# A hybrid decoder step: GLU, last projections and decode scores in one ordered list, and another row order for the decode score loads

## The chip, the core and the metric

The kernel runs on one NeuronCore of a Trainium2 chip. TensorE (PE) multiplies matrices into PSUM, VectorE (DVE), ScalarE (ACT) and GpSimd (POOL) do elementwise work, and SyncE's queue (SP) issues all DMA transfers of this kernel. Each engine works through its own instructions in order. The metric is the device time of one execution in microseconds (us); lower is better. All arithmetic is float32, with matmul operands split into a high and a low part, so that a product takes three matmul passes.

## The reference, cut to what matters

One layer of a decoder for a prompt of 1024 tokens and a decode batch of 8 sequences with 4 new tokens each. A projection gives `[x_ssm | z_ssm | q | k | v | z_attn]`. The state-space branch ends with a GLU; the attention branch of the decode rows attends to a cache of 1024 rows under three patterns.

```python
proj = _rmsnorm(h, norm_in_g) @ w_in
...
gl = g @ w_glu.astype(jnp.float32) + b_glu.astype(jnp.float32)
y_s = gl[..., :D_SSM] * jax.nn.sigmoid(gl[..., D_SSM:])
y_s = (y_s * jax.nn.silu(z_s.astype(jnp.float32))).astype(h.dtype)
y_s = _rmsnorm(y_s, norm_ssm_g)
...
offs = jnp.arange(window // dil + 1) * dil
idx = (l_ - t_ + jnp.arange(t_))[:, None] - offs[None, :]
...
s = jnp.einsum('bthe,btkhe->bhtk', q, kg) * (HEAD_DIM ** -0.5)
...
out = jnp.concatenate([y_s, y_a], axis=-1) @ w_out
```

with `DILATED_PATTERNS = ((128, 1), (512, 4), (2048, 16))`, `DEC_BATCH = 8`, `DEC_SEQ = 4`.

## The kernel before

The work runs in stages. First the prompt is normalised and transposed (`xT`), then the input projection goes block by block (`in_proj(blk)`, 12 blocks of 256 columns) between the eight groups of the state-space scan (`ssm(o)`). The change concerns the stage behind that.

**GLU** (lines 718 to 773). `w_glu` is loaded in four tiles `wst` and split into `wg`. For each pair `s0` of eight row groups and each of four column tiles `ct`, PE does 24 matmuls (L748) into two PSUM tiles, ACT takes tanh (L753) into `gb_`, of which there is one buffer, DVE gates (L754, L755), ACT squares (L759), and POOL adds the squares into `acc` (L760). The last two need `gb_`, so the next tanh waits for POOL's addition.

**Decode scores** (lines 811 to 838). For each batch `b` six tiles of 128 cache rows are loaded into `ct` (three buffers): tile 0 (L791), tile 1 (L793) and tiles 6 to 9 (L797). Tile 0 is transposed on PE (L822), split into `kh` and `kl`, and multiplied with the queries (L828, L829). For the other five POOL multiplies the tile with the query rows `dq` (L802, `dot`), and DVE reduces the product per head into `scd` (L803). `dq` has one buffer; its load (L835) spreads the four query rows over 128 partitions. `kh`, `kl` and the products share three buffers `dm`. The tiles are loaded so that query j stands on partitions 32j to 32j+31:

```python
SY.dma_start(c, src[b, 0:512, :].rearrange("(m r) c -> r m c", r=16)[0:DS])
...
SY.dma_start(c, src[b, 512:1024, :].rearrange("(m r j) c -> m j r c", r=32, j=DS)[t - 6])
...
SY.dma_start(qt, d_pd[:, b, 1024:1536].unsqueeze(1).to_broadcast([DS, 32, 512]))
```

**Last projections.** Blocks 6 and 10 (`REST_BLOCKS`, six groups of 24 matmuls each, L313, weights split at L141 and L142, results stored to `d_k` and `d_ga` at L381 and L373), then four tiles of `w_out`, then the softmax over the scores (`decode_ops`: transposes L914, softmax L921 to L967, transposes back L979), then block 11.

**What sets the order.** The code up to here is written straight down, and the framework's own scheduler interleaves it: it places each instruction on its engine, and SP's transfers too, by its own estimate. `decode_ops` and the attention behind it (`values_ops`, `scores_ops`, `micro_ops`, `out_ssm_ops`) are lists of steps of a class `Plan`: each step has an engine, a cost, a priority, the steps it needs and the buffers it takes and gives (`tokens`). `Plan.run` goes through the list as if each engine took that long, always takes the step that can start first (the smaller priority among equals), and emits the steps in the order of their starts. In the attention this order is fixed on PE, DVE, ACT and POOL (`manual_schedule`).

Of the kernel before, what the change touches and what calls it, by code (L numbers as in the profile page):

```python
# [95 lines left out]
BANKS = {"fo": 3, "tp": 4, "ss": 7, "ops": 3, "kt": 3}  # L96
# [6 lines left out]
def hymba_kernel(ctx: ExitStack, tc: tile.TileContext, I, O):  # L103
# [600 lines left out]
    fin = [rp]  # L704

# [9 lines left out]
    wg = wgo.tile([128, 2, 4, 1024], F32R, tag="wg", name="wg")  # L715
    for k in range(4):
        s = st.tile([128, 1024], F32, tag="st", name="wst")
        SY.dma_start(s, I["w_glu"][k * 128:(k + 1) * 128, :])
        split(wg[:, 0, k, :], wg[:, 1, k, :], s)

    bg, hb = wk([128, 8], "bg"), wk([128, 4], "hb")
    SY.dma_start(bg, I["b_gluT"])
    V.tensor_scalar(hb, bg[:, 4:8], 0.5, 1.0, op0=OP.mult, op1=OP.mult)
    for k in range(4):
        SY.dma_start(z[:, k], d_y[k])
    sums = ps_tile([128, 8], "so")
    dsum = ps_tile([128, NT], "so")
    all1 = wk([128, 128], "all1")
    GP.memset(all1, 1.0)
    for s0 in range(0, 8, 2):  # L730
        w, ts = W if s0 < DS else NC, slice(s0, s0 + 2)
        yh, yl = (wk([128, 4, 2, W], n, F32R, b) for n, b in (("yh", 2), ("yl", 1)))
        for k in range(0, 4, 1 if s0 == 0 else 2):
            k = slice(k, k + (1 if s0 == 0 else 2))
            split(yh[:, k], yl[:, k], z[:, k, ts])
        yT = yh, yl
        acc = wk([128, 2, W], "acc", bufs=1)[:, :, :w]
        for ct in range(4):
            gt = wk([128, 2, W], "gt", bufs=3)[:, :, :w]
            SY.dma_start(gt, d_gs[ct, :, ts, :w])  # L740
            pp = []
            for hf, tag in enumerate(("ss", "ss")):
                p = ps_tile([128, 512], tag)[:, :2 * w].rearrange("p (s k) -> p s k", k=w)
                i = 0
                c = 512 * hf + 128 * ct
                for kt in range(4):
                    for a, b in PASSES:
                        T.matmul(p, wg[:, b, kt, c:c + 128], yT[a][:, kt, :, :w], start=(i == 0), stop=(i == 11))  # L748
                        i += 1
                pp.append(p)  # L750
# [54 lines left out]
    def query():  # L805
        return dk([128, 512], "dq", bufs=1)
# [825 lines left out]
```

## Time and profile before

| | us |
|---|---|
| time, median of 3 runs | 816.28 (814.58 to 818.41) |
| the profiled execution's own time | 816.68 |
| its span in the trace | 814.8 |
| PE busy | 703.5 (86% of the span) |
| DVE / ACT / POOL busy | 561.2 / 363.3 / 347.0 |
| chain that ended last, by kind | PE 37%, DMA 28%, DVE 17%, ACT 5%, POOL 4% |

The profile gives each engine's busy time, the clock that PE was granted (1.00 is 2.4 GHz, 0.50 is 1.2 GHz), the chain of work that ended last, and for each instruction what ended its wait. The largest single entry of the chain is the load of decode cache tiles, `ct<-in_cache_k_dram`, with 12.8% of the span. The stage of the change lies between 324 and 535 us.

### The profile page before, as it was taken

The numbers are of one execution on the slowest core, as the hardware profiler recorded it, in microseconds if no ns is written. First come the engines' busy times: TensorE is split into PE (matmuls) and PEld (weight loads), VectorE is DVE, ScalarE is ACT, GpSimd is POOL, SyncE is SP. The second block draws the span as 40 slices with busy tenths as digits, with TensorE's granted clock in tenths as the row PEclk, the third lists the DMA queues.
The fourth block names the chain that finished last, engine by engine and source line by source line (L and its number), as shares of the span: only waits on it lengthen the run. The fifth ranks groups of instructions, "written<-read, shape, count | busy, mean of one in ns | idle before, by whom it ended". The sixth has DMA issues, their size and how long they took to land.

```text
span 814.8 us, 12780 instructions
## 1 busy us (share of the span) xinstructions
PE 703.5 (86%) x4286; PEld 634.6 (78%) x4286; DVE 561.2 (69%) x1249; ACT 363.3 (45%) x814; POOL 347.0 (43%) x315
## 2 busy tenths in 40 slices
PE   7999989598989999587767668989989999989996
PEld 6999878588978899576767657867757777778896
DVE  5995787879786762444435355649789999996286
ACT  6653244223425244322212222228667787772163
POOL 2506663544654410133433334016567687740022
PEclk9999999798999999796898878989999999999999
DMA  8424142322332444554434354368898788305423
GB/s 282 162 79 139 37 135 85 119 63 67 110 123 93 156 132 147 151 143 160 127 119 142 114 175 139 108 183 243 251 254 247 218 234 242 101 6 181 132 84 130
DMA packets 77362, 118.38 MB, mean 145 GB/s; under 512 B 14544, under 2 KB 42704, under 8 KB 77296
## 3 DMA queue, kind: packets, MB, share of 16 engines
q1 hardware_dynamic: 77296, 117.56, 46.8%
q8 instruction: 34, 0.56, 0.3%
q14 instruction: 32, 0.26, 0.1%
HBM read 85.73 MB, written 30.62 MB: 143 GB/s over the span
## 4 chain that ended last, share of the span: by engine, by line
PE 37%; DMA 28%; DVE 17%; issue 5%; ACT 5%; POOL 4%; SPq 3%; DVEq 0%; POOLq 0%; ACTq 0%
DMA ct<-in_cache_k_dram 13%; PE mm L313 13%; PE mm L293 4%; DMA ct<-in_cache_v_dram 4%; PE ss L293 3%; PE tp L293 3%; PE fo L1418 3%; DMA wst<-in_w_in_dram 3%; PE so L684 2%; POOL dm L802 2%; DVE pm L1269 2%; PE ops L1323 2%; DVE vl L1107 2%; DMA dq<-d_pd 2%; DVE pl L1315 2%
## 5 line engine op out<-in xcount | busy, mean ns | idle before, releaser
L313 PE MATMUL mm<-xT,win 128*128 128x352 f32 x1440 | 262.9, 338 | 23.4 <-DVE eq L380 16.7
L313 PEld LDWEIGHTS mm<-xT,win 128*128 128x128 f32 x1440 | 242.4, 198 | 28.0 <-issue 14.6
L802 POOL TENSOR_TENSOR dm<-ct,dq 128x512 f32<-128x512 f32 x40 | 52.5, 1312 | 124.2 <-DMA ct<-in_cache_k_dram 80.4
L803 DVE TENSOR_REDUCE scd<-dm 128x8 f32<-128x512 f32 x40 | 27.4, 684 | 78.0 <-POOL dm L802 78.0
L748 PE MATMUL ss<-yh,wg 128*128 128x272 f32 (+1 forms) x256 | 56.4, 317 | 19.8 <-DVE z L754 17.1
L1289 POOL TENSOR_SCALAR pm<-pm,rd 128x128 f32<-128x128 f32 (+3 forms) x64 | 52.0, 818 | 39.1 <-DVE rd L1285 27.6
L748 PEld LDWEIGHTS ss<-yh,wg 128*128 128x128 f32 x256 | 46.5, 217 | 22.4 <-DVE z L754 18.7
L142 DVE SCALAR_TENSOR_TENSOR win<-wst,gin,win 128x256 fp32r<-128x256 f32 x96 | 55.2, 617 | 11.0 <-ACT win L141 10.7
L141 ACT ACTIVATE win<-wst,gin 128x256 fp32r<-128x256 f32 x96 | 43.7, 502 | 33.7 <-DMA wst<-in_w_in_dram 29.8
L1281 ACT ACTIVATE pm<-pm,mn 128x128 f32<-128x128 f32 (+3 forms) x64 | 49.2, 770 | 15.3 <-DVE mn L1269 14.9
L1315 DVE TENSOR_TENSOR pl<-tp,ph 128x512 fp32r<-128x512 f32 (+1 forms) x80 | 49.7, 628 | 5.7 <-ACT ph L1312 5.4
L1418 PE MATMUL fo<-wo,gh 128*128 128x512 f32 x192 | 51.1, 408 | 0.0
L293 PE MATMUL mm<-win,xT 128*128 128x256 f32 x384 | 50.4, 286 | 0.1
L1308 PE MATMUL tp<-ident,pm 128*128 128x128 f32 x288 | 47.0, 283 | 1.5 <-DVE mn L1269 1.2
L293 PEld LDWEIGHTS mm<-win,xT 128*128 128x128 f32 x384 | 46.9, 189 | 0.5 <-ACT xT L138 0.4
L1312 ACT ACTIVATE ph<-tp 128x512 fp32r<-128x512 f32 (+1 forms) x80 | 42.9, 543 | 2.7 <-PE tp L1308 1.2
L1269 DVE CUSTOM_DVE_ANT_0 pm<-ss,maskp 128x512 f32<-128x512 f32 (+2 forms) x64 | 36.9, 580 | 9.6 <-DMA qt<-d_q 4.8
L1266 PE MATMUL ss<-ka,qt 128*128 128x512 f32 (+2 forms) x96 | 38.1, 398 | 4.3 <-DMA ka<-d_k 2.4
L1308 PEld LDWEIGHTS tp<-ident,pm 128*128 128x128 f32 x288 | 35.6, 145 | 7.5 <-DVE mn L1269 1.9
L1418 PEld LDWEIGHTS fo<-wo,gh 128*128 128x128 f32 x192 | 35.4, 194 | 6.6
L1103 ACT ACTIVATE vh<-ct 128x512 fp32r<-128x512 f32 x48 | 30.0, 626 | 23.1 <-DMA ct<-in_cache_v_dram 10.9
L379 ACT ACTIVATE eq<-mm 64x352 fp32r<-64x352 f32 (+1 forms) x48 | 21.5, 448 | 41.7 <-DVE eq L380 20.6
(399 smaller groups left out, 1584.7 us busy)
## 6 DMA issues: line engine op xcount, KB each, us to landing
wst<-in_w_in_dram SPq DMA_DIRECT2D x24, 512.0 KB
ct<-in_cache_k_dram SPq DMA_DIRECT2D x48, 256.0 KB
ct<-in_cache_v_dram SPq DMA_DIRECT2D x48, 256.0 KB
xt<-in_x_prompt_dram SPq DMA_DIRECT2D x8, 512.0 KB
wst<-in_w_out_dram SPq DMA_DIRECT2D x8, 512.0 KB
xres<-in_x_prompt_dram SPq DMA_DIRECT2D x8, 512.0 KB
qt<-d_q SPq DMA_DIRECT2D x16, 256.0 KB
qw<-d_q SPq DMA_DIRECT2D x32, 128.0 KB
```

What stands on the lines that cost most here:

```text
L141: S.activation(hi, src, AF.Copy, scale=scale)
L142: V.scalar_tensor_tensor(lo, src, scale, f(hi), op0=OP.mult, op1=OP.subtract)
L293: T.matmul(out, lhs(a, kt), w(b, kt)[:, c0:c0 + cn], start=(n == 0), stop=(n == 3 * ktn - 1))
L313: T.matmul(p, w(b, kt)[:, c * 128:c * 128 + 128], x(a, kt), start=(n == 0), stop=(n == 23))
L748: T.matmul(p, wg[:, b, kt, c:c + 128], yT[a][:, kt, :, :w], start=(i == 0), stop=(i == 11))
L802: GP.tensor_tensor(out=m, in0=kt, in1=qt, op=OP.mult)
L1269: V.tensor_tensor_reduce(out=x.pm[:, 512 * c:512 * c + w], in0=x.p[c][:, :w], in1=maskp[:, (7 - i) * 128 + 512 * c:(7 - i) * 128 + 512 * c ...
L1281: S.activation(x.pm[:, :n], x.pm[:, :n], AF.Exp, scale=-1.0, bias=x.mn[:, nch - 1:nch], accum_out=x.dn)
L1289: a = op(PO, 0.02 + n * 0.0012, lambda: GP.tensor_scalar(x.pm[:, :n], x.pm[:, :n], x.rd, 1.0, op0=OP.mult, op1=OP.mult), pr, [a], give=["rd"])
L1308: T.transpose(x.p[:, n * 128:n * 128 + 128], o.rows[2 * m + u].pm[:, j * 128:j * 128 + 128], ident)
L1315: V.tensor_tensor(out=x.l[:, :w], in0=x.p[:, :w], in1=f(x.h[:, :w]), op=OP.subtract)
L1418: T.matmul(o.f[hf], o.g[u][:, i, k], wo[0][:, j, 2 * u + k, hf * 512:hf * 512 + 512], start=(u + k + n == 0), stop=(u + k + n == 4))
```

## The change

Three things change together.

1. **Row order of the decode score tiles.** Query j now stands on each partition 4m+j. Tiles 6 to 9 are then 128 neighbouring rows, tile 1 and the query rows are loaded with the 32 as the outer count, and the places that undo the order (`ev`, `tr3`, `copy3`, the constant `sel3`) follow. `ct` has five buffers in place of three.
2. **One list of steps.** GLU, decode scores, blocks 6, 10 and 11, the `w_out` tiles and `decode_ops` become steps of one `Plan`, with costs and priorities, and the order is fixed on all five queues, SP's too.
3. **PSUM.** The pool of eight equal banks is opened before the GLU instead of after block 11; the GLU may hold up to four banks (`gl`).

The instructions are otherwise the same: same matmuls, same elementwise operations, same bytes.

```diff
+BANKS = {"fo": 3, "tp": 4, "ss": 7, "ops": 3, "kt": 3, "mm": 3, "gl": 4}
 REST_BLOCKS = (6, 10)
+LAST_BLOCK = 11
...
+    KT = 5
     def cache_tile(src, b, t):
-        c = dk([128, 512], "ct", bufs=3) if fin[0] else gk([128, 512], "ct", bufs=CT)
+        c = dk([128, 512], "ct", bufs=KT) if fin[0] else gk([128, 512], "ct", bufs=CT)
         if t == 0:
             SY.dma_start(c, src[b, 896:1024, :])
         elif t == 1:
-            SY.dma_start(c, src[b, 0:512, :].rearrange("(m r) c -> r m c", r=16)[0:DS])
+            SY.dma_start(c, src[b, 0:512, :].rearrange("(m r) c -> m r c", r=16)[:, 0:DS])
         elif t < 6:
             SY.dma_start(c, src[b, 510 + t:1024:4, :])
         else:
-            SY.dma_start(c, src[b, 512:1024, :].rearrange("(m r j) c -> m j r c", r=32, j=DS)[t - 6])
+            SY.dma_start(c, src[b, 128 * t - 256:128 * t - 128, :])
...
-        SY.dma_start(qt, d_pd[:, b, 1024:1536].unsqueeze(1).to_broadcast([DS, 32, 512]))
+                SY.dma_start(x.q, d_pd[:, b, 1024:1536].unsqueeze(0).to_broadcast([32, DS, 512]))
+            q = op(DM, 1.0, query, pr - 9.5, [], take=["dq"])
...
+                a = op(DM, 1.0, load, p - 10, [], take=["ct"])
+                a = op(PO, 1.3, mul, p, [a, q], take=["dm"], give=["ct"] + ["dq"] * (n == 4))
+                ends.append(op(VE, 0.69, red, p, [a], give=["dm"]))
...
+                a = op(AC, 0.5, tanh, pr + 1, [mm[1]], take=["gb"], give=["gl"])
+                b = op(VE, 0.5, gate, pr + 1, [mm[0], g], give=["gl", "gt"])
+                a = op(VE, 0.45, gate2, pr + 1, [a, b], give=[] if ct else ["gb"])
+                a = op(AC, 0.43, square, pr + 1, [a, acc], take=[] if ct else ["acc"])
+                if ct:
+                    a = op(PO, 0.78, more, pr + 1, [a], give=["gb"])
...
+    plan.tokens = {**BANKS, "pp": 7, "ct": KT, "dm": 3, "dq": 1, "st": 2, "ev": 2, "gh": 0, "w": 12, "y": 2, "gt": 3, "gb": 1, "acc": 1}
+    glu_last, glu_end = glu_ops(5.0)
+    keys_end = keys_ops(6.0)
+    k6 = proj_ops(REST_BLOCKS[0], -40, 1)
+    rows_end = rows_ops(70, k6)
+    proj_ops(REST_BLOCKS[1], 70, 1.0)
...
+    opened = op("", 0.0, open_decode, 0, [glu_end, *keys_end])
+    soft = decode_ops(-100, 0.1, op(DM, 0.1, lambda: None, 0, [opened, *rows_end]))
+    proj_ops(LAST_BLOCK, 95, 1)
+    with tc.manual_schedule(engines={nc.tensor.engine, nc.vector.engine, nc.scalar.engine, nc.gpsimd.engine, nc.sync.engine}):
+        plan.run()
...
-    in_proj(11)
     xst.close()
-    pst.close()
...
-    sel3 = (np.arange(128)[:, None] // 32 == np.arange(4)[None, :]).astype(np.float32)
+    sel3 = (np.arange(128)[:, None] % 4 == np.arange(4)[None, :]).astype(np.float32)
```

Where it moves instructions, three places. The first is PE at the start of the stage, behind the last matmuls of block 9 (L406 before, L407 after). Before, the GLU's products (`ss<-yh,wg`) come at once:

```order
L406 MATMUL mm<-win,xT_97 64x256 x16
L748 MATMUL ss<-yh,wg 128x272 x2
L748 MATMUL ss<-yl,wg 128x272
L748 MATMUL ss<-yh,wg 128x272 x2
L748 MATMUL ss<-yl,wg 128x272
```

and after, block 6 (`mm<-xT,win`, 96 matmuls up to the first transposes of a cache tile):

```order
L407 MATMUL mm<-win,xT_97 64x256 x16
L1022 MATMUL mm<-xT_97,win 128x352 x2
L1022 MATMUL mm<-xT_98,win 128x352
L1022 MATMUL mm<-xT_97,win 128x352 x2
L1022 MATMUL mm<-xT_98,win 128x352
```

So 96 of block 6's 144 matmuls moved ahead of the GLU; the other 48 stand between the GLU's first groups, where before all of block 6 was spread over the GLU. Block 10 comes when the GLU is nearly done, and block 11 runs around the softmax: behind the first transposes of the finished scores 120 of its matmuls still stand, behind the first of those that turn the softmax back 36.

The second place is SP in the decode scores, at the second batch: `ct` are the cache tiles, `dq` the query rows, `d_k` a store of block 6, `gt` a GLU operand. Before:

```order
L791 DMA ct<-in_cache_k_dram 128x512
L851 DMA nv<-d_pd 64x1x64 x2
L740 DMA gt<-d_gs 128x272
L793 DMA ct<-in_cache_k_dram 128x1x512
L835 DMA dq<-d_pd 128x1x512
L797 DMA ct<-in_cache_k_dram 128x1x512
L851 DMA nv<-d_pd 64x1x64 x2
L219 DMA wst<-in_w_in_dram 128x1024
```

After, from the last `w_glu` tiles and the first batch's loads on:

```order
L755 DMA wst<-in_w_glu_dram 128x1024 x2
L890 DMA ct<-in_cache_k_dram 128x512
L1071 DMA d_k<-eq 128x352 x2
L966 DMA dq<-d_pd 128x1x512
L892 DMA ct<-in_cache_k_dram 128x1x512
L896 DMA ct<-in_cache_k_dram 128x512 x2
L1071 DMA d_k<-eq 128x352 x2
L1084 DMA d_pd<-pd 32x256
L1086 DMA out_k_sample_dram<-pd 32x256
L800 DMA gt<-d_gs 128x272
```

Each load of a tile is now one run of 128 rows (`128x512`) but for tile 1 and `dq`, and block 6's stores stand among the first loads, two of them (`128x320 x2`) ahead of the two `w_glu` tiles shown.

The third place is POOL, the multiplications of the scores (`dm<-ct,dq`) and the GLU's additions (`acc<-acc,gb`). Before:

```order
L802 TENSOR_TENSOR dm<-ct,dq 128x512 x5
L760 TENSOR_TENSOR acc<-acc,gb__3858 128x272
L760 TENSOR_TENSOR acc<-acc,gb__3892 128x272
L802 TENSOR_TENSOR dm<-ct,dq 128x512 x4
L760 TENSOR_TENSOR acc<-acc,gb__3926 128x272
L802 TENSOR_TENSOR dm<-ct,dq 128x512 x2
L760 TENSOR_TENSOR acc<-acc,gb__4003 128x272
```

After:

```order
L977 TENSOR_TENSOR dm<-ct,dq 128x512 x6
L832 TENSOR_TENSOR acc<-acc,gb__4134 128x272
L977 TENSOR_TENSOR dm<-ct,dq 128x512 x4
L832 TENSOR_TENSOR acc<-acc,gb__4241 128x272
L832 TENSOR_TENSOR acc<-acc,gb__4323 128x272
L977 TENSOR_TENSOR dm<-ct,dq 128x512 x5
L832 TENSOR_TENSOR acc<-acc,gb__4426 128x272
L832 TENSOR_TENSOR acc<-acc,gb__4491 128x272
```

The additions now stand mostly behind the five multiplications of a batch, where POOL has no query rows for the next one yet; the first stands behind the first multiplication of the second batch.

## Rows read from the trace of the kernel before

**Rows 1.** Busy time by stretch: engines with counts, PE clock, DMA share, GB/s.
```profile
324.00:535.00 211.00, 157.35 (x959) 148.60 (x958) 100.31 (x212) 54.78 (x129) 62.92 (x53) 0.85 0.44 137
330.00:475.00 145.00, 103.06 (x652) 98.77 (x650) 61.95 (x114) 34.90 (x85) 51.26 (x44) 0.84 0.44 134
510.00:535.00 25.00, 23.52 (x143) 21.64 (x143) 15.26 (x38) 6.74 (x18) 0.00 (x0) 1.00 0.27 93
```
**Rows 2.** The chain that ended last, 386 to 407: start, us, what.
```profile
388.71 8.44 DMA ct<-in_cache_k_dram
397.28 1.28 POOL dm L802
398.57 6.36 DMA dq<-d_pd
```
**Rows 3.** Groups on POOL, 324 to 535: count, busy, mean ns, idle before by releaser.
```profile
L802 POOL TENSOR_TENSOR dm<-ct,dq 128x512 f32<-128x512 f32 x40 | 52.5, 1312 | 124.2 <-DMA ct<-in_cache_k_dram 80.4 <-DMA dq<-d_pd 32.7 <-DVE dm L139 6.7
```
**Rows 4.** Timeline around 393: start, us, engine, line, what, wait before.
```profile
392.63 0.34 SPq L791 DMA_DIRECT2D ct<-in_cache_k_dram  x1
393.24 1.35 DVE L139 TENSOR_TENSOR yl<-z,yh 128x544 fp32r<-128x544 f32 x2
393.92 1.79 POOL L802 TENSOR_TENSOR dm<-ct,dq 128x512 f32<-128x512 f32 x1 [0.58 <-DMA ct<-in_cache_k_dram]
397.96 1.09 PE L822 MATMUL tp<-ident,ct 128*128 128x128 f32 x4 [4.35 <-DMA ct<-in_cache_k_dram]
```
**Rows 5.** Tile dq: count, duration min/median/max in ns, first and last start.
```profile
L802 POOL TENSOR_TENSOR dm<-ct,dq x40: 1260/1278/1793, 337.6 to 504.1; 128x512 f32<-128x512 f32 x40
L835 SPq DMA_DIRECT2D dq<-d_pd x8: 522/538/584, 326.5 to 480.6; - x8
```
**Rows 6.** Timeline of PE, the stage's first and last matmuls and two stretches at full clock.
```profile
321.94 1.99 PE L406 MATMUL mm<-win,xT 128*64 128x256 f32 x16
...
334.08 0.26 PE L828 MATMUL tp<-qhl,dm 128*128 128x16 f32 x1
334.30 0.26 PE L828 MATMUL tp<-qhl,dm 128*128 128x16 f32 x1
...
350.71 0.41 PE L748 MATMUL ss<-yh,wg 128*128 128x272 f32 x2
351.08 0.41 PE L748 MATMUL ss<-yh,wg 128*128 128x272 f32 x2
...
530.77 3.80 PE L313 MATMUL mm<-xT,win 128*128 128x352 f32 x22
534.42 0.27 PE L401 MATMUL tp<-ident,pdT 128*32 128x128 f32 x1
```
**Rows 7.** Groups on PE, 324 to 535, the three that waited or ran most.
```profile
L313 PE MATMUL mm<-xT,win 128*128 128x352 f32 x432 | 85.7, 350 | 3.2 <-ACT win L141 1.5 <-DVE ev L372 1.4 <-DVE ge L372 0.2
L748 PE MATMUL ss<-yh,wg 128*128 128x272 f32 (+1 forms) x256 | 56.4, 317 | 19.8 <-DVE z L754 17.1 <-ACT wg L138 1.3 <-DVE wg L139 0.7
L822 PE MATMUL tp<-ident,ct 128*128 128x128 f32 x32 | 6.9, 353 | 24.9 <-DMA ct<-in_cache_k_dram 24.9
```
**Rows 8.** Timeline of one wait of the GLU, PE and POOL.
```profile
374.02 1.26 POOL L802 TENSOR_TENSOR dm<-ct,dq 128x512 f32<-128x512 f32 x1 [3.69 <-DMA ct<-in_cache_k_dram]
375.24 0.76 POOL L760 TENSOR_TENSOR acc<-acc,gb__3926 128x272 f32<-128x272 f32 x1
...
370.02 0.82 PE L748 MATMUL ss<-yh,wg 128*128 128x272 f32 x2 [5.84 <-DVE z L754]
370.87 0.65 PE L748 MATMUL ss<-yh,wg 128*128 128x272 f32 x2
371.55 0.65 PE L748 MATMUL ss<-yh,wg 128*128 128x272 f32 x2
```
**Rows 9.** Timeline, last reduction of the scores and last step of the softmax.
```profile
505.40 0.69 DVE L803 TENSOR_REDUCE scd<-dm 128x8 f32<-128x512 f32 x1 [3.96 <-POOL dm L802]
521.57 1.37 DVE L967 TENSOR_TENSOR sc<-sc,sdn 64x1168 f32<-64x1168 f32 x1
```

More of the change, by code (lines that the diff above doesn't have):

```diff
@@ L704, in hymba_kernel @@
     fin = [rp]
+    pst.close()
+    ps[0] = ctx.enter_context(tc.tile_pool(reuse_waits="tile", name="ps2", bufs=1, space=PSUM))
+    banks = {}
     def dk(shape, tag, dt=F32, bufs=1):
@@ L868, in hymba_kernel @@
+    class Box:
+        pass
     plan = Plan(nc)
@@ L892, in hymba_kernel, with weight_ops, load, hi @@
-    class Box:
-        pass
-    def decode_ops(t0, dt_):
+    bg, hb = wk([128, 8], "bg"), wk([128, 4], "hb")
+    SY.dma_start(bg, I["b_gluT"])
+    V.tensor_scalar(hb, bg[:, 4:8], 0.5, 1.0, op0=OP.mult, op1=OP.mult)
+    both = ps_tile([128, 8 + NT], "so")
+    sums, dsum = both[:, :8], both[:, 8:]
+    all1 = wk([128, 128], "all1")
+    GP.memset(all1, 1.0)
+    wg = wgo.tile([128, 2, 4, 1024], F32R, tag="wg", name="wg")
+    def weight_ops(src, out, prio, dt_, deps, scale=None):
+        ends = []
+        for k in range(4):
+            x = Box()
+            def load(k=k, x=x):
+                x.s = st.tile([128, 1024], F32, tag="st", name="wst")
+                SY.dma_start(x.s, src(k))
+            def hi(k=k, x=x):
+                S.activation(out()[:, 0, k, :], x.s, AF.Copy, scale=scale(k) if scale else 1.0)
+            def lo(k=k, x=x):
+                if scale:
+                    V.scalar_tensor_tensor(out()[:, 1, k, :], x.s, scale(k), f(out()[:, 0, k, :]), op0=OP.mult, op1=OP.subtract)
+                else:
+                    V.tensor_tensor(out=out()[:, 1, k, :], in0=x.s, in1=f(out()[:, 0, k, :]), op=OP.subtract)
+            p = prio + dt_ * k
+            a = op(DM, 1.7, load, p - 8, deps, take=["st"])
+            a = op(AC, 1.1, hi, p, [a])
+            ends.append(op(VE, 1.3, lo, p, [a], give=["st"]))
+        return ends
@@ new lines, in hymba_kernel, with rows_ops, load, load_wo @@
+    newr = [nr.tile([64, DS, E], F32, name=n) for n in ("nq", "nk", "nv")]
+    def rows_ops(pr, k6):
+        ends = []
+        for n, off in enumerate((1024, 1536, 2048)):
+            def load(n=n, off=off):
+                for j in range(DS):
+                    SY.dma_start(newr[n][:, j], d_pd[j, :, off:off + 512].rearrange("b (h e) -> b h e", e=E))
+            ends.append(op(DM, 1.2, load, pr, [k6] if n == 1 else []))
+        return ends
+    wo = []
+    def load_wo(k, out):
+        s = st.tile([128, 1024], F32, tag="st", name="wst")
+        SY.dma_start(s, I["w_out"][k * 128:(k + 1) * 128, :])
+        split(out[:, 0, k % 4, :], out[:, 1, k % 4, :], s, scale=gnorm[:, k:k + 1])
```

437 lines of the change are left out of this document (281 added, 156 removed).

## The prediction

> **What bounds the kernel now.** I read the busy time by stretch first. In the stage of the change, 324 to 535, PE is busy 157.35 of 211 us and its granted clock is 0.85; between 330 and 475 it is 103.06 of 145 at 0.84, while at the end, 510 to 535, it is nearly full at 1.00 [rows 1]. The DMA engines are at a share of 0.44 there, DVE at 100.31, ACT at 54.78, POOL at 62.92 us [rows 1]: no engine is the limit in this stage, something is waited for. The chain that ended last says what: a cache tile lands 8.44 us after its issue begins, POOL multiplies for 1.28 us, the query rows take 6.36 us, and so on [rows 2]. POOL does 40 multiplications of 1.28 us (52.5 us busy) and sits idle 124.2 us before them, 80.4 us on cache tiles and 32.7 us on query rows [rows 3]. The first multiplication starts at 337.6, the last at 504.1 [rows 5]: 166.5 us for eight batches, 20.8 us each, of which only 6.4 are multiplication. With three buffers and six tiles a batch, two round trips of a load fit that.
>
> PE hangs on this in two ways: it waits 24.9 us for the tile that it transposes, and 17.1 us in the GLU for DVE [rows 7]. The second is POOL's queue again: at 370.02 PE has waited 5.84 us; the GLU's addition stands in POOL's queue behind a multiplication that waited 3.69 us for its tile and starts at 374.02, so the addition ends at 376.0 [rows 8]. Behind that wait PE runs at the low one of its two clock levels (1.2 GHz): three GLU matmuls in 0.68 us (370.87 to 371.55), against 0.37 at 2.4 GHz (350.71 to 351.08) [rows 6, 8].
>
> **The floor.** What PE has to do between the last matmul of block 9 (321.94 + 1.99 = 323.9) and the last of block 11 (534.4) [rows 6], at the full clock: 432 projection matmuls at 0.166 us (22 from 530.77 to 534.42) = 71.7; 384 GLU matmuls at 0.125 = 48.0; the key products, 64 at 0.11 (two in 0.22 from 334.08 to 334.30) = 7.0, and 32 transposes at half of 1.09/4 us, since that row stands at the low clock, = 4.4; and of the 959 records 47 others, transposes and sums, at up to 0.22 = at most 10.3, of which I take 8.5 [rows 1, 4, 6]. Together 139.6. The stage now takes 534.4 - 323.9 = 210.5, so PE loses 70.9 us to waits and the low clock. That is all that can be won here. Nothing is removed: instructions and bytes stay.
>
> **Part 1, row order and five buffers.** What a load costs when its rows lie in one run is in the trace: tile 0, issued at 392.63, releases PE's transposes at 397.96, 5.3 us, in the midst of the others that take 8.4 [rows 2, 4]. Tiles 6 to 9 get that form. Tile 1 and the query rows get another, 32 outer steps of 4 rows, which no row shows; bounds: 5.3 us (like tile 0) and 8.4 (like now; the query rows 6.4 now [rows 2]). I take 6.4 for the query rows, the nearest row, and their gain as zero. The Trainium skill says more ("DMA: Bandwidth & Descriptors", section "Why a DMA increments its semaphore by 16 and not by 1"): a transfer is spread over the largest number of DMA engines, up to 16, that divides the slowest dimension of both sides. By it the old loads, with 4 outermost, would use four engines and all new ones sixteen; the query rows would land in tile 0's 5.3 us, and the chain below would end 9 us sooner, with the same total, since PE ends last in it.
>
> With five buffers a batch's tiles are there before its query rows, which have one buffer and can be asked for only after the fifth multiplication of the batch before. So a batch costs 5 x 1.28 = 6.4 us [rows 5] plus 6.4 for the rows plus about 0.5 for the issue of a tile ahead of it on SP (a load's issue takes 0.34 to 0.54 [rows 4, 5]): 13.3 us in place of 20.8. Start: SP's new list has two stores of block 6 ahead of the last GLU weights and the first tile, and two more ahead of the first query rows. The second pair needs 48 matmuls of block 6 (323.9 + 8.0 = 331.9) and the eviction, some 1 us; rows landing 6.4 later give a first multiplication at 339. Eight batches without the last gap: 339 + 8 x 13.3 - 6.9 = 438.5, and 0.7 for the last reduction [rows 9]. At 8.4 us for the rows: 453.
>
> **Part 2, the softmax.** From the end of the last reduction (506.1) to the end of the normalised scores (522.9) it is 16.8 us [rows 9], so 456. Behind the transposes that turn it back 36 matmuls of block 11 are listed, 6.0 us, and a us of transposes: PE's last block could end at 463. The PE floor ends at 323.9 + 139.6 = 463.5. The two meet; the 120 matmuls listed behind the first score transposes (20 us) cover the softmax. If the chain is 10 us later that cover is gone and the end moves with it, us for us.
>
> **Part 3, one list.** It fills PE's first wait: before, the GLU began with two of its four weight tiles missing; now 96 matmuls of block 6 (16 us) stand there, to 340. SP's order makes the last two GLU weights wait for the first eviction of block 6 (about 329); with a 6 us landing and two 1.2 us splits they are ready near 339: hidden. What the list does not remove:
> - GLU waits. An addition on POOL waits behind up to five multiplications (6.4 us), the first one also behind the query rows' 6.4. PE is two groups ahead at most (four `gl` banks, 2 x 24 x 0.125 = 6 us). Bounds: 0, and the 17.1 us of now [rows 7]. The GLU lasts four to five batches, the waits for tiles go: I take half, 8.5.
> - The three `dm` buffers: while `kh` and `kl` hold two, multiplications run one by one; and half of block 6's weights wait for block 9's buffers. Bounds 0 and 6.7 (the wait for DVE in [rows 3]); I take 2.
> - Low clock behind such waits: between 0 and about 17 us (157.35 busy against 139.6); with a fifth of the waits I take 3.5.
>
> Sum of the losses 14. An order that is fixed on SP also puts what is listed behind a store behind that store's producer; loads behind it start later and with them PE's transposes. That lies in the 14 as long as it is one or two us each.
>
> **The sum.** 70.9 - 14 = 57 us less. The profiled execution's own time is 816.68, the median 816.28, so both bases give the same: 816.7 - 57 = 760. The stages ahead and behind stay; of the cache loads of values behind, 8 of 48 get the new tile 1 form, off PE's path as far as the trace shows; I count zero.
>
> **Rivals.**
> - *PE never waits.* The losses are near nothing: 816.7 - 70.9 = 746, at best 744. For it: the planned order has no filler in the GLU, as if none were needed. Against: the plan gives a load 1 us plus 2, the trace 5.3 and more [rows 4]. 0.13.
> - *POOL's chain ends last.* The multiplications get longer or the rows land late. In the trace one multiplication takes 1.79 us instead of 1.28 while DVE splits `yl` beside it [rows 4, 5]. If every one did, a batch is 13.3 + 2.6 = 15.9 and the scores end at 460; plus 16.8 and 7.0 gives 484, and with the low clock behind PE's wait (5) 489: 45 us less, 772. With rows at 8.4 too 18 per batch, and 787. The Trainium skill has a rule for it ("SBUF — State Buffer", section "Who interferes with whom"): a DVE instruction with two SBUF inputs and a GpSimd one that reads SBUF exclude each other for a whole instruction; DVE's work, now 100 us in 211, would be 100 in 150. The row at 393.92 agrees with it, the median of 1.278 says that it is rare. 0.17.
> - *The fixed order convoys.* Eight transposes of tiles and 16 GLU groups on PE wait 2 us each for something that came later than planned, 48 us in all instead of 14: 816.7 - 23 = 794. For it: real landings are twice the planned ones, and no engine can go round a late one any more. Against: most of its waits overlap. 0.13.
> - *The loads are no faster* (the change doesn't do what it says). Then 8.4 us for rows, five tiles per 10 us: the chain ends at 454, and PE at 478, all but the forecast: 762. It would show in the loads, not the time; it is inside the forecast's case.
> - *Slower than before.* SP is one queue, now in a fixed order with 40-odd stores and operand loads between the tiles. If they hold it so that a batch takes 22 us, the scores end at 339 + 8 x 22 - 7 = 508, and 508 + 17 + 7 = 532: that is the point from which nothing is won; at 25 us a batch, 556 and 838. It needs 9 us of SP waits per batch on top; the trace's whole batch is 20.8 with two round trips in it. 0.04 for slower, 0.02 for the same.
>
> **How the numbers follow.** Forecast 760, its own case (750 to 770) 0.51; 744 to 750 0.13; 770 to 787 0.17; up to 800 0.13; the rest 0.06. The range 744 to 790 leaves out about 0.15. One measurement of this kernel tells 0.5%, 4 us, from no change: faster 0.94, same 0.02, slower 0.04.
>
> **What would show it.** Right: cache tiles land in 4 to 6 us, POOL's first to last multiplication spans about 100 us instead of 166.5, PE's clock in the stage is above 0.95, block 11 ends near 478, and the attention behind is unchanged but shifted. Wrong: POOL still idle for tiles; PE idle in front of L932 or L809 by more than 25 us in all; the end of the softmax more than 6 us ahead of or behind PE's last block; or a stage behind that grew.

## The result, and the profile after

The changed kernel takes 744.15 us (median, 740.57 to 745.37) against 817.35 for the kernel before beside it: a ratio of 0.910 (0.906 to 0.915), 73 us less. The forecast was 760, 57 us less. Measured once more, beside other runs, the changed kernel took 741.69, a ratio of 0.908 (0.905 to 0.911). The profiled execution took 745.36 with a span of 743.6.

| us | before | forecast | after |
|---|---|---|---|
| last matmul of block 11 ends | 534.4 | 478 | 471.9 |
| from there to the first matmul of the last projection (L293, L294) | 217.5 | unchanged | 207.1 |
| from there to the end | 62.9 | unchanged | 64.6 |

So 62.5 us went in the stage of the change, and some 10 in the attention behind it, whose work is the same but for the form of one load; the last stage took 1.7 us longer.

The busy time by stretch of the changed kernel, over the stage (its line in [rows 1] has the same columns: length, PE, PE's weight loads, DVE, ACT, POOL, clock, DMA share, GB/s):

```profile
324.00:472.00 148.00, 139.91 (x961) 135.88 (x959) 107.24 (x211) 58.13 (x131) 64.69 (x53) 0.97 0.66 213
```

PE is busy 139.91 of 148 us; it was 157.35 of 211 at a clock of 0.85. The groups of that stretch (count, busy, mean ns, idle before by releaser), POOL's multiplications first, then PE's, as in [rows 3, 7]:

```profile
L977 POOL TENSOR_TENSOR dm<-ct,dq 128x512 f32<-128x512 f32 x40 | 52.8, 1350 | 46.6 <-DMA ct<-in_cache_k_dram 27.6 <-DMA dq<-d_pd 7.0 <-ACT gb__4686 L829 3.9
L809 PE MATMUL gl<-yh,wg 128*128 128x272 f32 (+1 forms) x256 | 50.8, 297 | 0.0
...
L946 PE MATMUL tp<-qhl,dm 128*128 128x8 f32 x32 | 7.4, 255 | 2.1 <-DVE dm L939 2.0
...
L932 PE MATMUL tp<-ident,ct 128*128 128x128 f32 x32 | 5.0, 278 | 1.2 <-DMA ct<-in_cache_k_dram 1.2
...
L845 PE MATMUL so<-ones,acc 128*128 128x1 f32 x16 | 2.6, 264 | 2.4 <-POOL acc L832 2.4
```

PE's 24.9 us of waiting for the tile to transpose are 1.2, the GLU's 17.1 for DVE are 0.0. POOL's idle time for tiles fell from 80.4 to 27.6 us, and that is one single wait, ahead of the first multiplication. POOL's line on the tile `dq` (count, duration, first and last start), as in [rows 5], and the timeline of the turn of one batch, as in [rows 2]:

```profile
L977 POOL TENSOR_TENSOR dm<-ct,dq x40: 1262/1290/1768, 344.4 to 437.3; 128x512 f32<-128x512 f32 x40
```

```profile
353.39 0.53 SPq L966 DMA_DIRECT2D dq<-d_pd  x1
...
357.77 1.28 POOL L977 TENSOR_TENSOR dm<-ct,dq 128x512 f32<-128x512 f32 x1 [4.40 <-DMA dq<-d_pd]
...
359.73 5.23 POOL L977 TENSOR_TENSOR dm<-ct,dq 128x512 f32<-128x512 f32 x4
```

Forty multiplications now span 92.9 us instead of 166.5. Between first and last start lie 7.8 batches: 11.9 us each. In the turn shown the query rows land 4.4 us after their issue began; the tiles are there when they do.

### The profile page after: what moved, and what is told of

The parts are those of the page before. It is cut to its first block, busy times and chain, and to the rows that moved or that the text cites. A ratio compares the mean times of both kernels' runs of the same rounds, so it can differ in the third digit from the quotient of the medians.

```text
span 743.6 us, 12795 instructions
## 1 busy us (share of the span) xinstructions
PE 683.3 (92%) x4286; PEld 623.8 (84%) x4286; DVE 564.1 (76%) x1249; ACT 366.8 (49%) x814; POOL 348.0 (47%) x315
## 4 chain that ended last, share of the span: by engine, by line
PE 51%; DVE 24%; DMA 8%; issue 6%; ACT 5%; POOL 5%; SPq 1%; DVEq 0%; POOLq 0%; ACTq 0%
PE mm L314 13%; PE mm L294 6%; PE fo L1670 4%; PE ss L294 3%; PE tp L294 3%; PE ops L1575 3%; DVE pm L1521 3%; POOL dm L977 3%; PE so L685 3%; PE tp L1560 2%; DVE vl L1359 2%; PE ss L1518 2%; DVE pl L1567 2%; PE fo L1365 2%; DVE win L143 2%
## 5 line engine op out<-in xcount | busy, mean ns | idle before, releaser
L314 PE MATMUL mm<-xT,win 128*128 128x352 f32 x1008 | 178.1, 334 | 15.1 <-DVE eq L381 13.7
L314 PEld LDWEIGHTS mm<-xT,win 128*128 128x128 f32 x1008 | 168.2, 196 | 16.8 <-issue 14.0
L1022 PE MATMUL mm<-xT,win 128*128 128x352 f32 x432 | 76.4, 331 | 0.4 <-DVE win L1004 0.2
L977 POOL TENSOR_TENSOR dm<-ct,dq 128x512 f32<-128x512 f32 x40 | 52.8, 1350 | 46.6 <-DMA ct<-in_cache_k_dram 27.6
L1022 PEld LDWEIGHTS mm<-xT,win 128*128 128x128 f32 x432 | 70.5, 192 | 1.1 <-DVE win L1004 0.9
L1533 ACT ACTIVATE pm<-pm,mn 128x128 f32<-128x128 f32 (+3 forms) x64 | 49.3, 772 | 13.2 <-DVE mn L1521 12.1
L294 PE MATMUL mm<-win,xT 128*128 128x256 f32 x384 | 51.7, 290 | 0.1
L809 PE MATMUL gl<-yh,wg 128*128 128x272 f32 (+1 forms) x256 | 50.8, 297 | 0.0
L294 PEld LDWEIGHTS mm<-win,xT 128*128 128x128 f32 x384 | 48.1, 194 | 0.5 <-ACT xT L139 0.4
L1560 PE MATMUL tp<-ident,pm 128*128 128x128 f32 x288 | 45.1, 275 | 0.5 <-DVE mn L1521 0.5
L143 DVE SCALAR_TENSOR_TENSOR win<-wst,gin,win 128x256 fp32r<-128x256 f32 x72 | 43.9, 650 | 1.9 <-ACT win L142 1.4
L809 PEld LDWEIGHTS gl<-yh,wg 128*128 128x128 f32 x256 | 41.9, 198 | 0.0
L1518 PE MATMUL ss<-ka,qt 128*128 128x512 f32 (+2 forms) x96 | 36.1, 378 | 2.5 <-DMA ka<-d_k 1.8
L809 PE MATMUL gl<-yl,wg 128*128 128x272 f32 (+1 forms) x128 | 37.6, 294 | 0.0
```

Of the source, the lines that this page charges most:

```text
L143: V.scalar_tensor_tensor(lo, src, scale, f(hi), op0=OP.mult, op1=OP.subtract)
L294: T.matmul(out, lhs(a, kt), w(b, kt)[:, c0:c0 + cn], start=(n == 0), stop=(n == 3 * ktn - 1))
L314: T.matmul(p, w(b, kt)[:, c * 128:c * 128 + 128], x(a, kt), start=(n == 0), stop=(n == 23))
L809: T.matmul(p, wg[:, b, kt, c:c + 128], o.y[a][:, kt, :, :o.w], start=(n == 0), stop=(n == 11))
L977: GP.tensor_tensor(out=y.m, in0=y.c, in1=x.q, op=OP.mult)
L1022: T.matmul(x.p, o.w[kt][:, b, c * 128:c * 128 + 128], xT[a][:, kt, 352 * k:352 * k + 352], start=(kt == 0 and j == 0), stop=(kt == 7 and j ...
```

## The experiments

Each ratio below is taken against the kernel before, measured beside that run; runs of different groups are compared by their ratios and not by their times. The changed kernel's ratio is 0.909, the mean of its two.

### Which part of the change it is

The first four kernels separate three causes: the row order, the list with its buffers, and the attention's instruction order, which differs between the two kernels because a step of the older list that the attention waits for is named there by its place in that list.

`d1_new_rows` is the kernel before with the new row order alone:

```diff
-            SY.dma_start(c, src[b, 0:512, :].rearrange("(m r) c -> r m c", r=16)[0:DS])
+            SY.dma_start(c, src[b, 0:512, :].rearrange("(m r) c -> m r c", r=16)[:, 0:DS])
...
-            SY.dma_start(c, src[b, 512:1024, :].rearrange("(m r j) c -> m j r c", r=32, j=DS)[t - 6])
+            SY.dma_start(c, src[b, 128 * t - 256:128 * t - 128, :])
...
-        SY.dma_start(qt, d_pd[:, b, 1024:1536].unsqueeze(1).to_broadcast([DS, 32, 512]))
+        SY.dma_start(qt, d_pd[:, b, 1024:1536].unsqueeze(0).to_broadcast([32, DS, 512]))
```

> The kernel before with the new row order alone: three buffers, the framework's own order. If the round trips of the loads carry the stage (two per batch, each 8.4 + 1.3 us, now about 5.3 + 1.3): a batch takes 14 us instead of 20.8, the scores end 45 us earlier, and with the last blocks' weights still to come 775 to 785 us. If the one list is what is needed: 800 us or more.

It took 747.89 us, 0.916 (0.910 to 0.923), 27 us below the lower end of what was expected. `c1_old_rows` is the opposite: the changed kernel with these lines set back, so list, fixed order and five buffers alone.

> The changed kernel with the old row order of the score tiles, value tile 1 and query rows (query j on partitions 32j to 32j+31; the steps that undo it as before); five buffers and the one list stay. If the list and the buffers carry the gain and PE covers the slower loads, as the prediction's case of loads that are no faster says: 755 to 765 us, POOL's first to last multiplication about 115 us. If the row order carries most: 780 us or more, with the multiplications spread over 140 us or more and PE waiting for tiles.

It took 819.88, 1.003 (1.000 to 1.006): nothing won. With the old rows the list and its buffers are worth nothing, and the rows without the list bring nearly everything. The two kernels that exchange the attention's order, in the changed kernel and in the one before:

```diff
+    gh_order[0][8] = 26
```

> The changed kernel, with the attention stage's steps in the order they had before the change (one line sets the number of an earlier step, on which the planner's greedy choice hangs; no instruction is added or removed). The stage of the change is untouched. Theory A, the 8.6 us that the attention stage lost in the profile come from its changed order: 752 to 755 us, and the stretch from the last matmul of block 11 to the first of the last stage is 215 to 218 us again instead of 207. Theory B, they come from the faster loads of the eight value tiles or from chance: 742 to 746 us and 207 us.

745.32, 0.913 (0.908 to 0.918). The other way round, with 2 in the kernel before:

> The kernel before, with the attention stage's steps in the order of the changed kernel and nothing else. Theory A (the order): 806 to 809 us. Theory B (loads or chance): 815 to 818 us.

817.17, 1.002 (0.999 to 1.006). The order of the attention's instructions moves nothing that shows.

### Why the rows: four DMA engines are full

What the first four left was a sharper form of "the loads are faster"; the expectations below call it theory E. The rate of the DMA engines in 40 slices of 0.4 us, with their mean share in tenths above it, in the kernel before from 484 to 500:

```profile
DMA  2239568995322222222889899522222222223458
GB/s 98 99 143 384 147 164 338 348 333 154 102 102 102 102 102 102 102 102 102 236 257 308 277 352 346 191 102 102 102 97 102 102 102 108 103 106 107 149 166 210
```

The chain that ended last in the same stretch (start, us, what):

```profile
484.71 11.11 DMA wst<-in_w_in_dram
```

The rate falls to 102 GB/s and stays there, at a share of a quarter, while the chain waits 11.11 us for a weight load. A quarter of sixteen engines is four, 25.5 GB/s each: four are full, and twelve idle. The old loads have 4 as their outermost count. The mean share of 0.44 in [rows 1] hid it, and the prediction's "no engine is the limit in this stage" was wrong for these four.

From this follows a price. A batch has six such loads of 262 KB, 393 KB on each of four engines, and some 80 KB of each engine's share of all else (19.0 MB moved from 340 to 480, of it 10.1 in such loads; the rest is 0.56 MB per engine in 6.7 batches): 473 KB at 25.5 GB/s is an estimated 18.5 us of the 20.8 that a batch took (the prediction divided 166.5 us by eight; over 7.8 batches, as above, it is 21.3). More buffers cannot change that. Two kernels vary the outermost count with the same rows' size and number, `k8_scores` and `k2_scores` (the count is 2 there):

```diff
-            SY.dma_start(c, src[b, 0:512, :].rearrange("(m r) c -> m r c", r=16)[:, 0:DS])
+            if fin[0]:
+                SY.dma_start(c, src[b, 0:512:4, :].rearrange("(r g) c -> g r c", g=8))
...
-            SY.dma_start(c, src[b, 128 * t - 256:128 * t - 128, :])
+            SY.dma_start(c, src[b, 128 * t - 256:128 * t - 128, :].rearrange("(r g) c -> g r c", g=8))
...
-                SY.dma_start(x.q, d_pd[:, b, 1024:1536].unsqueeze(0).to_broadcast([32, DS, 512]))
+                SY.dma_start(x.q, d_pd[0, :, 1024:1536].unsqueeze(1).to_broadcast([8, 16, 512]))
```

> The same with 2 outermost steps. (Again other rows of the same number and size; the scores are wrong, work and bytes are the same.) Theory E: two engines carry the score loads: (6 x 131 KB + 78 KB) / 22.7 GB/s = 38 us a batch, eight of them 297 us from POOL's first to last multiplication instead of 93; the stage and the time are some 205 us longer: 950 us (920 to 980). Rival (slow landing of a scattered load, hidden or not by five buffers): as with 4 outermost steps, 811 or less; and a rival in between (each load lands later, in proportion, but loads overlap freely): a batch is 6.4 us of multiplications and some 13 us of landing, 20 us, about 815.

> The changed kernel, whose score loads (tile 1, tiles 6 to 9, query rows) get 8 outermost steps. (Rows and query rows of the same number and size, in another order and for tile 1 and the queries other rows, so the scores are wrong; work and bytes are the same.) Theory E: eight engines carry them; a batch needs (6 x 32.8 KB + 78 KB) / 22.7 GB/s = 12.1 us on those, about what a batch takes in the changed kernel (11.9): 748 us (744 to 755), the loads land in two parts' time more, and POOL's first to last multiplication spans 93 to 105 us. Rival (any regrouping of rows into a few outer steps costs what the old one cost, whatever the number of engines): 811.

2 steps gave 925.38 us, 1.133 (1.124 to 1.141), within the expected range; 8 gave 760.99, 0.930 (0.925 to 0.936), 6 us above it. The same two lines of the DMA view, for 2 steps from 560 to 576, then for 8 from 430 to 446:

```profile
DMA  1111111111111111111111111111111649999999
GB/s 51 51 51 51 51 51 51 51 51 51 51 46 51 51 51 51 51 51 51 51 51 51 51 51 51 51 51 51 51 51 51 113 123 379 389 307 328 287 323 292
```

```profile
DMA  7479878999999998654554555555555588969699
GB/s 148 128 195 205 230 271 251 312 312 225 282 282 287 266 277 282 241 220 189 210 195 189 195 184 179 200 200 200 200 205 200 205 310 308 391 240 287 251 336 289
```

The floor is 51 with 2 steps, 102 with 4 and about 200 with 8: always some 25 GB/s an engine. The engines' mean share is 0.13 with 2 steps (560 to 572 us), 0.26 with 4 (`c1_old_rows`, 481 to 486) and 0.52 with 8 (438 to 442): two, four and eight of sixteen. The semaphore of each load tells the same: between its issue and its landing the trace has 3 events with 2 steps, 5 with 4, 9 with 8 and 16 with 16, for each of the 48 score loads of these runs; in the changed kernel, with 32 or 128 outermost steps, it has 16. `k16_scores` is the control, the same regrouping with 16 steps:

> The control of the runs with 2 and 8 outermost steps: the same regrouping of the score loads (tile 1, tiles 6 to 9, query rows) with 16 outermost steps. (Rows in another order, for tile 1 and the queries other rows; the scores are wrong, work and bytes are the same.) Theory E: all sixteen engines carry them as in the changed kernel: 742 us (738 to 747), POOL's span 90 to 95 us. Rival (regrouping costs by itself, apart from the number of engines, which would explain that 8 steps came out at 761 instead of 748): 750 or more.

It took 747.92, 0.915 (0.910 to 0.920), between its forecast and its rival: three of its four executions took about 748 us, the profiled one 740.13. The intervals of the changed kernel (0.906 to 0.915 and 0.905 to 0.911) touch this one, so a cost of the regrouping itself is not shown and, at 0.006, could be 5 us; it is not the 0.080 of 4 steps. The line of POOL's multiplications on the tile `dq`, for 2, 4 (`c1_old_rows`), 8 and 16 steps:

```profile
L980 POOL TENSOR_TENSOR dm<-ct,dq x40: 1260/1262/1744, 348.5 to 616.3; 128x512 f32<-128x512 f32 x40
```

```profile
L977 POOL TENSOR_TENSOR dm<-ct,dq x40: 1255/1264/1745, 348.8 to 501.3; 128x512 f32<-128x512 f32 x40
```

```profile
L980 POOL TENSOR_TENSOR dm<-ct,dq x40: 1255/1286/1770, 343.7 to 450.3; 128x512 f32<-128x512 f32 x40
```

```profile
L980 POOL TENSOR_TENSOR dm<-ct,dq x40: 1274/1289/1771, 342.3 to 434.8; 128x512 f32<-128x512 f32 x40
```

| outermost steps | KB per engine and batch | at 25.5 GB/s, us | a batch measured, us |
|---|---|---|---|
| 2 | 786 + 80 | 34.0 | 34.3 |
| 4 | 393 + 80 | 18.5 | 19.6 |
| 8 | 197 + 80 | 10.9 | 13.7 |
| 16 | 98 + 80 | 7.0 | 11.9 |

With 2 and 4 the engines set the batch. With 8 and 16 they don't: there it is for the most part the query rows, the chain that the prediction built. With 8 steps the rows are issued when a batch's last multiplication ends (in one case 1.5 us later), land after 6.4 us in the median, and in the second to eighth batch the first multiplication starts less than 0.2 us behind that. With five multiplications of 1.3 us these are 13.0 of the 13.7. The forecast let a batch stay near 12 us, as if eight loaded engines landed the rows as fast as sixteen do, in 4.6 us.

The Trainium skill states this as advice ("DMA: Bandwidth & Descriptors", section "Rules for kernel authors"): an outermost dimension smaller than 16 confines the whole transfer to at most as many engines. The runs with 2, 4, 8 and 16 agree. The same page of the Trainium skill gives an engine, in its section "Specifications", about 27 GiB/s, 29 GB/s; here, with rows of 2 KB, it was 25.5, and the sums above go by that.

### The attention: one load in six

The value tile 1, 8 of the attention's 48 cache loads, has the new form too. `f1_value_tile_old` sets that load alone back, `k4_scores_old` all others:

```diff
-            SY.dma_start(c, src[b, 0:512, :].rearrange("(m r) c -> m r c", r=16)[:, 0:DS])
+            v = src[b, 0:512, :].rearrange("(m r) c -> m r c" if fin[0] else "(m r) c -> r m c", r=16)
+            SY.dma_start(c, v[:, 0:DS] if fin[0] else v[0:DS])
```

> The changed kernel, with one load set back: the value tile 1 of the attention behind (8 of its 48 cache loads) again has 4 as its outermost count; all loads of the score stage stay new. (The value rows then stand in another order than their weights, so one pattern's output is wrong; instructions and bytes are the same.) Theory E (four engines full): a load with 4 outermost steps is carried by four of the sixteen DMA engines. It puts 65.5 KB on each of them instead of 16.4; for eight loads that is 393 KB more on each of the four. In the trace of before four engines carried about 3.17 MB each in 140 us (19.0 MB in all, of them 10.6 in narrow loads), 22.7 GB/s, so this is at most 17 us, and less as far as the other work there hides it: I expect the attention stage to grow by the 9 us by which it shrank, 754 us (750 to 758), and the landings of the other loads there to rise from about 5 to 7 us. Rival (the attention got shorter by another order or another neighbour): 745.

> The counterpart: the changed kernel with the loads of the score stage (tile 1, tiles 6 to 9, query rows) set back to 4 outermost steps, the value tile 1 left new. (The places that undo the row order stay those of the change, so the scores land in wrong places; instructions and bytes are the same.) Theory E: the score stage is bound by four full DMA engines, a batch takes (6 x 65.5 KB + 78 KB of other traffic) / 22.7 GB/s = 20.7 us, as before; only the attention's 9 us are won: 811 us (807 to 815). Together with the run of the value tile alone the two effects should add up to the 75 us between the changed kernel and the run with all loads old (819.9). Rival (the loads' slow landing counts, not their engines' load; five buffers hide it): about 762 to 775.

752.99, 0.921 (0.916 to 0.927), and 808.95, 0.989 (0.986 to 0.992). Against the changed kernel's 0.909 (mean of its two ratios) the value tile costs 0.012 and the scores 0.080; together 0.092, and the run with both old stands 0.094 above. The attention by stretch, before, after and with the value tile old:

```profile
534.50:752.00 217.50, 198.81 (x1135) 159.71 (x1134) 182.96 (x453) 147.56 (x317) 129.05 (x116) 0.96 0.69 199
```

```profile
472.00:679.00 207.00, 190.98 (x1134) 156.46 (x1133) 179.17 (x451) 148.81 (x318) 128.99 (x116) 0.98 0.68 207
```

```profile
471.90:687.00 215.10, 194.99 (x1133) 159.37 (x1132) 175.68 (x451) 148.33 (x318) 129.04 (x116) 0.96 0.70 199
```

All kernels with the old load there need 215 to 219 us for the attention, all with the new one 204 to 212. Other loads of that stage feel it as well: before, with the value tile old, and after, the wide value tiles (L795, L895, L894) land in 7.0, 6.1 and 5.2 us in the median, the key tiles `ka` in 7.4, 6.7 and 5.3. Of the 10.4 us between before and after only 2.7 are idle time of PE (18.7 against 16.0 in the lines above); for the rest PE is busy longer, at a clock of 0.96 against 0.98, and how these hang together was not taken apart. Who waits shows in ACT's group that splits the value tiles, before, after, and with the old load:

```profile
L1103 ACT ACTIVATE vh<-ct 128x512 fp32r<-128x512 f32 x48 | 30.0, 626 | 23.1 <-DMA ct<-in_cache_v_dram 10.9 <-PE fo L1113 9.0 <-PE tp L1308 2.1
```

```profile
L1355 ACT ACTIVATE vh<-ct 128x512 fp32r<-128x512 f32 x48 | 29.9, 623 | 8.0 <-PE fo L1365 3.3 <-DMA ct<-in_cache_v_dram 3.2 <-DVE vl L1359 1.1
```

```profile
L1356 ACT ACTIVATE vh<-ct 128x512 fp32r<-128x512 f32 x48 | 30.0, 625 | 17.5 <-DMA ct<-in_cache_v_dram 11.8 <-DVE vl L1360 3.0 <-PE fo L1366 1.3
```

### What is left: query rows, buffers, list

`m_query_old` sets the query rows' load alone back to 4 steps.

```diff
-                SY.dma_start(x.q, d_pd[:, b, 1024:1536].unsqueeze(0).to_broadcast([32, DS, 512]))
+                SY.dma_start(x.q, d_pd[:, b, 1024:1536].unsqueeze(1).to_broadcast([DS, 32, 512]))
```

> The changed kernel with the query rows alone loaded in 4 outermost steps again. (Each row then stands beside cache rows of another query, so the scores are wrong; work and bytes are the same.) Theory E: the four engines carry 65.5 + 5 x 16.4 + 78 = 225 KB a batch, at 22.7 GB/s 9.9 us, less than the 11.9 us that a batch takes in the changed kernel, so their load is not the bound. What is left is the chain that the prediction built: one buffer for the query rows, so a batch is five multiplications of 1.35 us, the landing and 0.5. The landing grows from 4.8 to about 7.5 us; a batch is then 14.3 us instead of 11.9, POOL's first to last multiplication 110 us instead of 93, the last block ends some 8 us later: 752 us (748 to 758). If the chain of the query rows is no bound either: 745, with POOL's span at 93.

755.60, 0.926 (0.921 to 0.931); POOL's span was 102.7 us (346.0 to 448.7), 13.2 a batch, the last block ended at 483.6. The query rows' landing does space the batches, as the prediction's chain has it, though by 1.3 us and not the 2.4 expected. The rows land in 6.7 us in the median of the eight, in the changed kernel in 4.6, and from the second batch on the first multiplication starts less than 0.2 us behind them. The profile itself puts only two of these waits, 6.9 us, down to the rows, so this rests on their landing times. This run does not separate the chain from the sharing of engines: with four of them carrying the rows, the tiles 6 to 9 too land in 5.1 us instead of 4.1, the GLU operands `gt` in 5.8 instead of 3.9.

Three buffers for the tiles in the changed kernel (`h1_three_buf`), and five in the kernel with the new rows alone (`e1_new_rows_5buf`):

```diff
-    KT = 5
+    KT = 3
```

```diff
-        c = dk([128, 512], "ct", bufs=3) if fin[0] else gk([128, 512], "ct", bufs=CT)
+        c = dk([128, 512], "ct", bufs=5) if fin[0] else gk([128, 512], "ct", bufs=CT)
```

> The changed kernel with three buffers for the cache tiles in place of five, in its list of steps (the planned order follows the number). Theory E: with wide loads a tile lands in some 4.7 us, so two round trips of three buffers with five multiplications are about 12 to 13 us a batch, as much as the query rows' chain; the buffers are worth little: 747 us (743 to 751). Rival (in a fixed order the buffers are what keeps POOL fed): POOL's span goes back to 120 us or more as in the run with the new rows alone, and the time to 755 or more.

> The kernel before with the new rows, as in the run with the rows alone (747.9 us), and five buffers in place of three; no list. Theory E: the rest of the loss there is PE's floor and the framework's order, not the buffers: 746 us (743 to 750), POOL's span falls from 120 to about 105 us without the time following. Rival (the buffers are the part that the list run gave on top): 744 or less.

> The changed kernel itself once more, as the measure for the three others of this call and for the part of the list: 744 us (741 to 747). If list, fixed order and five buffers are worth something beside the rows, it is some 3 us below the run with five buffers and without the list; if they are worth nothing, the same.

747.08, 0.915 (0.912 to 0.918); 753.78, 0.924 (0.920 to 0.928); and 741.69 for the changed kernel itself, 0.908. With three buffers POOL's span is 107.5 us, between the changed kernel's 92.9 and the 120 of the rival, and five buffers are worth some 5 us in the list. Without the list they shorten POOL's span from 119.8 to 101.9 us, and the time doesn't follow: POOL was no longer the bound. Then the list: `d2_new_rows_again` measures the rows alone a second time, and `g1_free_order` emits the changed kernel's list without fixing the engines' order:

```diff
-    with tc.manual_schedule(engines={nc.tensor.engine, nc.vector.engine, nc.scalar.engine, nc.gpsimd.engine, nc.sync.engine}):
-        plan.run()
+    plan.run()
```

> The new rows alone once more (three buffers, no list, the framework's order), beside the run without the fixed order. In the first call it was 747.9 (ratio 0.916 with an interval of 0.910 to 0.923), the changed kernel 0.908 (0.905 to 0.911) in another. If list and buffers are worth something: 747 to 751. If nothing: 742 to 745.

> The changed kernel with its list written out in the planned order, but the engines' order not fixed: the framework's scheduler places the instructions by its own estimate. If the fixed order is what the list's few us come from: 748 to 755, as with the rows alone or with five buffers. If the order in which the code is written is enough: 742.

751.25, 0.920 (0.916 to 0.924), and 752.44, 0.921 (0.917 to 0.926). So the list with its buffers, on top of the rows, is worth some 0.009 (0.918 to 0.909, means of two runs each), 7 us, and only with the fixed order: without that, the list is no better than no list.

Last, a second buffer for the query rows, paid for with one of the tiles', which should free POOL of the wait that is left:

```diff
-    KT = 5
+    KT = 4
...
-                x.q = dk([128, 512], "dq", bufs=1)
+                x.q = dk([128, 512], "dq", bufs=2)
...
-    plan.tokens = {**BANKS, "pp": 7, "ct": KT, "dm": 3, "dq": 1, "st": 2, "ev": 2, "gh": 0, "w": 12, "y": 2, "gt": 3, "gb": 1, "acc": 1}
+    plan.tokens = {**BANKS, "pp": 7, "ct": KT, "dm": 3, "dq": 2, "st": 2, "ev": 2, "gh": 0, "w": 12, "y": 2, "gt": 3, "gb": 1, "acc": 1}
```

> The changed kernel with a second buffer for the query rows and, to make room, four for the cache tiles in place of five. If the chain of the query rows (five multiplications, then the landing) is what spaces POOL's batches, as the prediction had it, POOL's first to last multiplication falls from 93 to about 75 to 80 us (40 multiplications of 1.35 and the GLU's additions). The time follows only as far as PE waited for it: PE's own work is 139.6 of the stage's 148 us, of which waits for POOL and the scores are some 4: 738 to 744 us. Rival (the four buffers or DMA become the bound): POOL's span stays at 90 or more, 745.

POOL's line on the tile `dq`, and the busy time of the stage's last stretch:

```profile
L977 POOL TENSOR_TENSOR dm<-ct,dq x40: 1261/1288/1775, 345.3 to 429.0; 128x512 f32<-128x512 f32 x40
```

```profile
440.00:481.30 41.30, 35.55 (x198) 33.24 (x197) 23.48 (x50) 14.05 (x28) 0.00 (x0) 0.88 0.39 126
```

POOL did get shorter, 83.7 us instead of 92.9, with no wait for query rows left; the time rose to 750.86, 0.921 (0.917 to 0.925). So the chain of the query rows was what spaced POOL, but the time did not follow as expected. The planner makes another order from the new numbers, and in it PE stands still more often: from 365 to 400 it is busy 30.05 us, in the changed kernel 32.28, and in the stretch shown 35.55 of 41.3, where the changed kernel has, from 440 to 472, 30.00 of 32. Block 11 ends at 481.3. The largest of PE's waits are 5.8 us in L1022 for DVE's splits of block 11's weights (L1004), 0.2 in the changed kernel. They fall at 448 to 457, where DVE does these splits between steps of the softmax. The clock from 440 on is 0.88 there and 1.00 in the changed kernel; from 365 to 400 it is 0.90 in both. None of the kernels tried beats the changed one.

## Why the prediction was wrong in size

The profiled kernel came out 71.3 us below the one before (816.68 against 745.36), where 57 were forecast. Of the 14 us between, 5.6 lie in the stage of the change and 10.4 in the attention; the last stage gave 1.7 back.

**The floor** held. PE's work was put at 139.6 us and the stage at no less; it took 148 with 139.91 busy, of 70.9 to be won it won 62.5.

**The losses of 14** were 8. The GLU's waits, half of the old 17.1, did not come: L809 waited 0.0, only the sums behind POOL's additions (L845) 2.4. The `dm` buffers cost the 2 that were taken (L946, 2.0), the tiles 1.2, and the clock was 0.97, above the 0.95 named. The step that failed here is "I take half": the additions do stand behind the multiplications, but in the listed order PE never came to stand on one of them in L809. Its ground was weak as well. The prediction read the wait in [rows 8] as POOL's queue, but PE's wait was over at 370.02, four us before the multiplication at 374.02. What released PE was DVE's gating (L754, at 369.47). It stood behind DVE's half of a weight split (L142, from 366.53, after 4.21 us of waiting for ACT's half), and ACT's half had waited for the weight tile:

```profile
365.99 1.70 ACT L141 ACTIVATE win<-wst,gin 128x256 fp32r<-128x256 f32 x4 [8.36 <-DMA wst<-in_w_in_dram]
```

So the longest of the GLU's waits, 5.84 of the 17.1 us, goes back to a load and not to an addition.

**Part 1** came out at the right place by luck, with two wrong numbers that cancel. The first multiplication started at 344.4 and not 339 (the first query rows were issued at 337.8), and a batch took 11.9 us and not 13.3, since the query rows' landing was not 6.4 but 4.4 (the row above; 4.6 in the median of the eight, from issue to last semaphore event); the last one ended at 438.6, forecast 438.5. What Part 1 drew from the Trainium skill was right in the engines, four for the old loads and sixteen for the new, and near in the landing of the query rows (5.3 against 4.6); the 6.4 that was taken instead, and "their gain as zero", were wrong.

**Part 2**: the reductions ended at 442.2 and the normalised scores at 466.8, forecast 439 and 456. The stretch from one to the other was taken from the kernel before as 16.8 us and was 24.6, since DVE did 10.9 us of other work in it, mostly evictions and weight splits (L1049, L762, L1004), where it had been 4.7. Behind it PE's last block ended 5 us later, so chain and floor did meet.

**"The stages ahead and behind stay … I count zero"** is the largest miss: 10 us. The 8 value loads were taken as off PE's path because the trace showed little PE waiting for them. With that load alone set back the time rises by 0.012, 10 us, and the other loads of the stage land later, on engines that they share with it. The prediction's sign "the attention behind is unchanged" failed by these 10 us.

**The rival "the loads are no faster"**, at 762 and "inside the forecast's case", was wrong by 58 us: with the old rows the list took 819.88, and still 808.95 with the value tile new. It let five tiles land per 10 us, 131 GB/s, where four engines carry 102. The old loads were priced by what one of them takes (8.4 us), as a latency that buffers hide. They were a queue. The prediction said that old loads would use four engines and put that into landing times only; 6 x 262 KB per batch through four engines was never worked out. So the sign of the change and the place of the waits were right, but not what makes the loads slow. The credit went to the buffers and the list, which with the old rows win nothing, and the one narrow load outside the list was sized at nothing.

The other rivals: POOL's chain did not end last (its multiplications went from 1312 to 1350 ns in the mean, not to 1790), and no convoy came. "PE never waits", at 746, was nearest, but by chance: PE did wait, 8 us in the stage, and the attention's gain made up for it.

## What to carry to other kernels

A low mean share of the DMA engines is no proof that they are free: look for stretches in which the rate lies flat on a part of the full rate, and divide bytes by the engines that carry them before pricing a wait as a latency. Put a count like the 16, 32 or 128 of these runs outermost in every large load; loads with 2, 4 or 8 also held up others in flight. When buffers are added to hide a landing, first ask whether the landing is a wait in a queue: here five buffers and the list won nothing (1.003) as long as four engines were full.

## What was not expected of the hardware

The flat rate is sharp: 51, 102 and 200 GB/s for 2, 4 and 8 outermost steps, 25 to 25.5 an engine. Narrow loads held up wide ones: the GLU operands `gt`, themselves spread over sixteen (16 semaphore events each), took 7.5 us in the median from issue to last event in the kernel before and up to 12.9, 3.9 after; in the changed kernel's list it was 13.2 with 2 outermost steps for the score loads, 10.2 with 4, 7.3 with 8 and 4.0 with 16. And eight narrow loads of 48 in the attention, with DMA at a mean share of 0.69, cost 10 us of 217 there.
